# Splitting the next weight unit ahead of the sums of one, in the first 52 units of a two-layer encoder

## The chip, the cores and the metric

The kernel runs on one core of one Trainium2 chip. The time is the device time of one execution in microseconds (us); of several executions the median is given. The core has a matrix engine (TensorE, PE in the profile), VectorE (DVE), ScalarE (ACT), GpSimd (POOL) and SyncE (SP). Each works through its own queue of instructions in order; semaphores hold an instruction until what it needs is done. In this kernel SyncE issues every load and store.

## The reference

Two layers on 256 tokens of width 2048. Each layer normalises its input, scales and shifts it by a vector made from a condition `c` (the modulation), and runs a mixer; then it normalises and modulates again and runs a gated MLP with a short convolution. Cut to what matters here:

```python
mod = c_act @ ada_w[l] + ada_b[l]                       # 6 vectors of 2048
sh_a, sc_a, gt_a, sh_m, sc_m, gt_m = split(mod, 6)
h = rmsnorm(x, norm_mix[l]) * (1.0 + sc_a) + sh_a
qa, ka, va, qb, kb, vb, ga, gb = split_cols(h @ w_in[l])
ya = window_attention(...) @ w_proj_a[l]
yb = neighbourhood_attention(...) @ w_proj_b[l]
merged = sigmoid(ga) * ya + sigmoid(gb) * yb
x = x + gt_a * (merged @ w_out[l])
```

Everything is float32. The output is x after both layers.

## The kernel before

**Weights as a stream.** The matrices are cut into blocks of 128 x 128 and laid out in the order in which they are used. Sixteen blocks are a *unit*: one transfer of 1 MB into one of four `raw` buffers (`unit`, L275 on; the load is L279). A product of float32 accuracy is made from two rounded parts of each operand: ScalarE casts the unit to a high part, half a unit at a time (L288), VectorE subtracts to get the low part (L289), both into one of four `hl` buffers, each half a unit. TensorE then does three matmuls for a block: high by high, high by low, low by high (L297 to L299 for sums by features, L355 to L357 for sums by tokens). A raw buffer is free again after the second subtraction, an hl buffer after its last matmul.

**The modulation.** One row of 128 outputs is one transfer of 1 MB (L219) into the same four raw buffers (three of the first rows have a place of their own, `OWN`) and one VectorE reduction (L220). Rows come in the order of `ADA_ORDER`: shift and scale of one kc, 128 of the 2048 channels, follow each other, so that two rows give what one kc of the first `h` needs. `done[0]` counts rows. `normed` (L427 to L432) then makes one kc of h: a product on VectorE (`ht`, L427), the high part on ScalarE (L430), the low part on VectorE (L431).

**The first layer's start.** Query, key and value need all 16 kc of h, but h comes kc by kc. So the 9 token sums (groups of 512 columns) and the 16 gate sums are done in three parts, each over the kc's that `K_ENDS` gives: a part's sums are put into `packs` or `ya` in the first part (ScalarE copies, L790 and L827) and added to them in the later ones (VectorE, L792 and L822). Units 0 to 12 are part one, 13 to 34 part two, 35 to 51 part three; units 52 on belong to the projections. In the third part the finished sums are normalised (`qk_rows`: L508, L516, L531 to L533), transposed on TensorE (L540), and the heads of the attention run beside it (`attend`: L552, L556, L572, L577, L583).

**What sets the order.** The program is written in one order, and a scheduler lays it out engine by engine: earlier written work has priority, but an instruction whose inputs come late by the scheduler's reckoning is passed by others. Background work is paced: after each unit `Stream.tick` lets every job in `bg` do as many steps as its rate says. `job0` (`ada_and_h`) is such a job: its steps load a modulation row or make a kc of h; its rate is `FIRST_RATE`, one for each part. `have_h` forces it on where a sum needs a kc that is not yet written. From unit 38 on `plan` fetches later rows at the pace of `ADA_PLAN_0`. `Stream.prefetch` writes a unit's load and split before it is its turn; before the change it does so for unit 0 and at the ends of later stages.

Of the kernel before, what the change touches and what calls it, by code (L numbers as in the profile page):

```python
# [19 lines left out]
KC = D // P  # L20
HEAD = 128
HA, GA, HB = 8, 2, 8
# [15 lines left out]


K_ENDS = [  # L40
    [([2, 2, 2, 3, 3, 4, 4, 4, 4], 6), ([8, 8, 9, 10, 10, 11, 10, 10, 12], 13), ([KC] * 9, KC)],
    [([KC] * 9, KC)],
]

# [14 lines left out]
ADA_PLAN_0 = [(38, 32), (58, 48), (76, 66), (84, 70), (98, 80), (108, 80), (231, 143)]  # L59
ADA_PLAN_1 = [(8, 143), (76, 166), (84, 168), (99, 176), (108, 176), (128, 184), (142, 192)]  # L60

FIRST_RATE = [1.1, 0.85, 0.7]
ENDING = 15

WARM_IN = [8, 12, 6]
# [64 lines left out]
def encoder(ctx: ExitStack, tc: tile.TileContext, a: dict, out: bass.AP):  # L130
# [69 lines left out]
    mods, amods, nrms, done = {}, {}, {}, {0: 0, 1: 0}  # L200
# [73 lines left out]
    def unit(l, u):  # L274

        raw = rawp.tile([P, UB * P], F32, name=f"w{l}_{u}", tag="raw")
        nc.sync.dma_start(raw[:], a["ws"][l, u])  # L279
        halves = []  # L280
        streamed = any(m == "w_in" and mo < GATE_A // P for m, _, mo in STREAMS[l][u * UB : (u + 1) * UB])
        at = OFF if streamed else 0
        for j in range(2):
            n = UB * P // 2
            hl = hlp.tile([P, 2 * n + ROW], F32R, name=f"hl{l}_{u}_{j}", tag="hl")
            hl = hl[:, at : at + 2 * n].rearrange("p (a n) -> p a n", a=2)
            r = raw[:, j * n : (j + 1) * n]
            nc.scalar.copy(hl[:, 0], r)  # L288
            nc.vector.tensor_tensor(out=hl[:, 1], in0=r, in1=hl[:, 0].bitcast(F32), op=ALU.subtract)  # L289
            halves.append(hl)  # L290
        return halves
# [9 lines left out]
    class Stream:  # L301
# [16 lines left out]
        def next_block(self):  # L318
            if self.at == UB:
                if self.ahead:  # L320
                    self.halves = self.ahead.popleft()
                else:
                    self.halves = unit(self.l, self.u)
                self.u, self.at = self.u + 1, 0
            j = self.at
            self.at += 1
            return self.halves[j // 8], j % 8
# [108 lines left out]
    def first_h(h):  # L436

        rbs = spread(roots(mean_sq), WARM_IN[2])
        yield from normed(0, 0, h, rbs)
# [60 lines left out]
    def qk_rows(pss, heads, rot, gain, dst, then):  # L500

        cols = 0
        n = heads * HEAD
        ss = sm.tile([P, 8], F32, name="qss", tag="qss")
        for t, ps in enumerate(pss):
            sq = at.tile([P, 512], F32, name="qsq", tag="qsq", bufs=1)
            nc.scalar.activation(out=sq[:, :n], in_=ps[:, cols : cols + n], func=AF.Square)
            nc.vector.tensor_reduce(  # L508
                out=ss[:, t * heads : (t + 1) * heads], in_=sq[:, :n].rearrange("p (h d) -> p h d", d=HEAD), axis=AX.X, op=ALU.add
            )  # L510
        rs = sm.tile([P, 8], F32, name="qrs", tag="qrs")
        rsqrt(rs[:, : 2 * heads], ss[:, : 2 * heads], HEAD, 2 * heads)
        def norm():
            qn = at.tile([P, 2, 4, HEAD], F32, name="qn", tag="qn", bufs=1)
            for t, ps in enumerate(pss):
                nc.vector.tensor_tensor(  # L516
                    out=qn[:, t, :heads],
                    in0=ps[:, cols : cols + n].rearrange("p (h d) -> p h d", d=HEAD),
                    in1=rs[:, t * heads : (t + 1) * heads].unsqueeze(2).broadcast_to([P, heads, HEAD]),
                    op=ALU.mult,  # L520
                )
            if rot is not None:
                x1, x2 = qn[:, :, :heads, :HALF], qn[:, :, :heads, HALF:ROT]
                tab = [rot[:, i].unsqueeze(2).broadcast_to([P, 2, heads, HALF]) for i in range(4)]
                tm = []
                for i in range(2):
                    z = ev.tile([P, S], F32, name=f"rt{i}", tag="z")
                    z = z[:].rearrange("p (i t h d) -> p i t h d", i=2, t=2, h=4)
                    tm += [z[:, 0, :, :heads], z[:, 1, :, :heads]]
                for i, src in enumerate((x1, x2, x2, x1)):  # L530
                    nc.vector.tensor_tensor(out=tm[i], in0=src, in1=tab[i], op=ALU.mult)  # L531
                nc.vector.tensor_tensor(out=x1, in0=tm[0], in1=tm[1], op=ALU.subtract)
                nc.vector.tensor_tensor(out=x2, in0=tm[2], in1=tm[3], op=ALU.add)  # L533
            bg.defer(lambda: turn(qn))

        def turn(qn):
            for t in range(2):
                ps = ax.tile([P, 4, P], F32, name="qtp", tag="ax")
                for h in range(heads):
                    nc.tensor.transpose(ps[:, h], qn[:, t, h], ident[:])  # L540
                nc.scalar.activation(
                    out=dst[:, :, t * P : (t + 1) * P], in_=ps[:, :heads], func=AF.Identity, scale=gain
                )
            then()

        bg.defer(norm)
# [50 lines left out]
    def ada_all():  # L597
        yield from gens[0]
        yield from gens[1]

    adas = ada_all()
# [9 lines left out]
    def need(l, n):  # L611

        while done[l] < n:
            next(adas)

    def ada_and_h(steps):

        for kc in range(KC):
            while done[0] < 2 * kc + 1:
                next(adas)  # L620
                yield
            next(adas)
            next(steps)
            yield

    for i in range(0, KC, 4):
# [48 lines left out]
    for l in range(L):  # L675
        st = Stream(l) if l == 0 else nxt
        mod = mods.get(l)
        if l == 0:
            h = led("h0_0")
            job0 = ada_and_h(first_h(h))  # L680
            while done[0] < 2:
                next(job0)
            st.prefetch(1)
            while done[0] < 2 * K_ENDS[0][0][0][0]:
                next(job0)
            mod = mods[0]
            bg.add(job0, FIRST_RATE[0])

# [19 lines left out]
        kTa, qTa = packs[0][:, 0:3:2], packs[0][:, 4:12]  # L708
# [61 lines left out]

        def have_h(part):

            while l == 0 and done[0] < 2 * part.stop:
                next(job0)

        for pi, (groups, gates) in enumerate(parts):
            last = pi == len(parts) - 1
            if l == 0:
                bg.pace(job0, FIRST_RATE[pi])
            for g, part in enumerate(groups):  # L780
                have_h(part)
                pss = st.tokens(h, part)
                if pi == max(0, len(parts) - 2) and g == 0:
                    gains, sink, cw, rots = small(l)
                dst = packs[g // 3][:, 4 * (g % 3) : 4 * (g % 3) + 4]
                rows = dst.rearrange("p (t a) s -> p t (a s)", t=2)
                if not last or pi > 0:
                    for t, ps in enumerate(pss):
                        if pi == 0:
                            nc.scalar.copy(rows[:, t], ps[:])  # L790
                        else:
                            nc.vector.tensor_tensor(out=rows[:, t], in0=ps[:], in1=rows[:, t], op=ALU.add)  # L792
                    pss = [rows[:, t] for t in range(2)]
                if not last:
                    continue

                def have(g=g):
                    ready[0] = g + 1

                vcol = {0: GA * HEAD, 4: 0, 7: 0}.get(g)  # L800
                if vcol is not None and pi == 0:
                    for t in range(2):
                        nc.scalar.copy(rows[:, t, vcol:], pss[t][:, vcol:])
                if g == 0:
                    qk_rows(pss, GA, rots[1], gains[:, 1:2], kTa, have)
                elif g < 3:
                    qk_rows(pss, 4, rots[0], gains[:, 0:1], dst, have)
                elif vcol is None:
                    qk_rows(pss, 4, None, gains[:, 3:4] if g in (3, 6) else gains[:, 2:3], dst, have)
                else:  # L810
                    have()
                if g == 2:
                    bg.add(job, ATT[l])


            have_h(gates)
            for mo in range(BARE[0] if l else 0, KC):

                def gate_a(ps):
                    src = ps  # L820
                    if pi > 0:
                        nc.vector.tensor_tensor(out=ya[:, mo], in0=ps, in1=ya[:, mo], op=ALU.add)  # L822
                        src = ya[:, mo]
                    if last:
                        nc.scalar.activation(out=ya[:, mo], in_=src, func=AF.Sigmoid)
                    elif pi == 0:
                        nc.scalar.copy(ya[:, mo], ps)  # L827

                st.features([hs[k] for k in gates], [gate_a])
# [223 lines left out]
```

## Time and profile before

| | |
|---|---|
| Time, median of 3 executions | 2702.55 us (2701.57 to 2703.78) |
| Time of the profiled execution | 2700.72 us |
| Its span, first to last instruction | 2698.9 us |
| Granted TensorE clock, mean | 0.997 |
| Bytes moved | 700.38 MB, 260 GB/s over the span |

The span in 40 equal slices of 67.5 us, from the page. A digit is the busy share of a slice in tenths; DMA is the mean share of the 16 DMA engines, the row under it what they moved. Units 0 to 28 run in the first three slices.

```profile
PE   8999999999999999999999999999999999999999
DVE  8897888897987888788886666658878866655664
DMA  8986678987677788788756656667847775555554
GB/s 348 351 337 242 228 271 327 354 302 265 235 298 292 284 303 285 291 298 289 297 210 255 240 203 239 226 245 253 295 176 283 296 259 193 189 202 188 191 199 141
```

How to read the views used below: a row of a wait list has who waited, for whom, the sum in us, how often, and the longest. A timeline row has the start and the length in us, the engine, the line, the tiles and, in brackets, the idle time before it and what ended that. A row of a group ends with its count, busy time in us, mean length in ns, and the idle time before its instructions.

### The profile page before, as it was taken

How to read it: one execution, taken by the hardware profiler on the slowest of the kernel's cores; microseconds unless marked ns; L12 is line 12 of the kernel's file. 1: busy time of each engine (PE TensorE's matmuls, PEld its weight loads, DVE VectorE, ACT ScalarE, POOL GpSimd, SP SyncE). 2: the span in 40 equal slices, each digit the busy share in tenths (PEclk: the TensorE clock that was granted, in tenths of full speed). 3: DMA queues.
4: the chain of work that ended last, by engine and by line, in shares of the span. 5: the costliest groups of instructions: out<-in, count | busy, mean ns of one | idle time of the engine just before them, and what ended most of it. 6: DMA issues, size and time to landing. Idle time of an engine off the chain costs nothing.

```text
span 2698.9 us, 50255 instructions
## 1 busy us (share of the span) xinstructions
PE 2665.7 (99%) x21128; PEld 2565.9 (95%) x21128; DVE 2089.7 (77%) x2909; ACT 1405.0 (52%) x2078; POOL 32.6 (1%) x24
## 2 busy tenths in 40 slices
PE   8999999999999999999999999999999999999999
PEld 5879799999999999999998889999999999999999
DVE  8897888897987888788886666658878866655664
ACT  4434685445753455355564556555565445543553
POOL 0000100000000000000000000000000000000000
PEclk9999999999999999999999999999999999999999
DMA  8986678987677788788756656667847775555554
GB/s 348 351 337 242 228 271 327 354 302 265 235 298 292 284 303 285 291 298 289 297 210 255 240 203 239 226 245 253 295 176 283 296 259 193 189 202 188 191 199 141
DMA packets 101892, 700.38 MB, mean 260 GB/s; under 512 B 12705, under 2 KB 15009, under 8 KB 17697
## 3 DMA queue, kind: packets, MB, share of 16 engines
q1 hardware_dynamic: 101666, 697.17, 69.9%
q8 instruction: 165, 2.70, 0.4%
q14 instruction: 61, 0.50, 0.1%
HBM read 695.03 MB, written 2.10 MB: 258 GB/s over the span
## 4 chain that ended last, share of the span: by engine, by line
PE 86%; DVE 8%; ACT 2%; DMA 2%; issue 2%; POOL 1%; SPq 0%; DVEq 0%; ACTq 0%; POOLq 0%
PE ps L297 25%; PE ps L299 25%; PE ps L298 25%; PE ps_t L356 3%; PE ps_t L357 3%; PE ps_t L355 3%; DVE hl L289 3%; DVE aw L220 2%; DMA aw<-in_aw 1%; ACT hl L288 1%; PE po L583 1%; PE sc L552 1%; POOL qrs L402 1%; PE tp L577 0%; DVE qn L516 0%
## 5 line engine op out<-in xcount | busy, mean ns | idle before, releaser
L289 DVE TENSOR_TENSOR hl<-w,hl 128x1024 fp32r<-128x1024 f32 x928 | 1130.0, 1222 | 376.0 <-ACT hl L288 374.8
L288 ACT CAST hl<-w 128x1024 fp32r<-128x1024 f32 x928 | 969.6, 1049 | 732.8 <-PE ps L299 493.9
L297 PE MATMUL ps<-h,hl 128*128 128x256 f32 x3328 | 923.6, 278 | 3.1 <-ACT hl L288 3.1
L299 PE MATMUL ps<-h,hl 128*128 128x256 f32 x3328 | 919.5, 277 | 1.3 <-DVE hl L289 1.3
L298 PE MATMUL ps<-h,hl 128*128 128x256 f32 x3328 | 920.6, 277 | 0.0
L297 PEld LDWEIGHTS ps<-h,hl 128*128 128x128 f32 x3328 | 625.6, 188 | 4.5 <-ACT hl L288 4.1
L299 PEld LDWEIGHTS ps<-h,hl 128*128 128x128 f32 x3328 | 624.8, 188 | 1.8 <-DVE hl L289 1.7
L298 PEld LDWEIGHTS ps<-h,hl 128*128 128x128 f32 x3328 | 625.5, 188 | 0.3
L220 DVE CUSTOM_DVE_ANT_0 aw<-aw,cact,ab 128x2048 f32<-128x2048 f32 x189 | 443.6, 2348 | 55.1 <-DMA aw<-in_aw 54.4
L355 PE MATMUL ps_t<-hl,h 128*128 128x512 f32 x576 | 226.0, 399 | 9.2 <-ACT h L430 4.6
L356 PE MATMUL ps_t<-hl,h 128*128 128x512 f32 x576 | 228.2, 396 | 3.8 <-DVE hl L289 3.3
L357 PE MATMUL ps_t<-hl,h 128*128 128x512 f32 x576 | 226.6, 394 | 0.0
L898 DVE SCALAR_TENSOR_TENSOR u<-ps,cw,u 128x255 f32<-128x255 f32 x304 | 146.2, 481 | 65.4 <-ACT u L896 61.1
L896 ACT ACTIVATE u<-ps,cw 128x256 f32<-128x256 f32 x152 | 85.6, 563 | 182.8 <-PE ps L299 182.6
L299 PE MATMUL ps<-merged,hl 128*128 128x256 f32 x512 | 141.6, 277 | 0.8 <-DVE hl L289 0.8
L298 PE MATMUL ps<-merged,hl 128*128 128x256 f32 x512 | 141.5, 276 | 0.0
L297 PE MATMUL ps<-merged,hl 128*128 128x256 f32 x512 | 141.5, 277 | 0.0
L298 PE MATMUL ps<-act_o,hl 128*128 128x256 f32 x512 | 141.4, 276 | 0.0
L299 PE MATMUL ps<-act_o,hl 128*128 128x256 f32 x512 | 141.3, 276 | 0.0
L297 PE MATMUL ps<-act_o,hl 128*128 128x256 f32 x512 | 141.2, 276 | 0.0
L355 PEld LDWEIGHTS ps_t<-hl,h 128*128 128x128 f32 x576 | 108.6, 189 | 34.2 <-ACT hl L288 6.9
L356 PEld LDWEIGHTS ps_t<-hl,h 128*128 128x128 f32 x576 | 109.2, 190 | 30.9 <-DVE hl L289 8.4
(213 smaller groups left out, 4562.2 us busy)
## 6 DMA issues: line engine op xcount, KB each, us to landing
w<-in_ws SPq DMA_DIRECT2D x464, 1024.0 KB, 4.9
aw<-in_aw SPq DMA_DIRECT2D x189, 1024.0 KB, 6.1
bias<-in_bias SPq DMA_DIRECT2D x16, 256.0 KB, 4.8
x<-in_xT SPq DMA_DIRECT2D x4, 512.0 KB, 5.4
aw_o<-in_aw SPq DMA_DIRECT2D x2, 1024.0 KB, 13.3
out<-x SPq DMA_DIRECT2D x16, 128.0 KB, 2.4
aw_b<-in_aw SPq DMA_DIRECT2D x1, 1024.0 KB, 15.1
cw<-in_cw SPq DMA_DIRECT2D x2, 176.0 KB, 6.0
```

What stands on the lines that cost most here:

```text
L220: nc.vector.tensor_tensor_reduce(out=raw[:], in0=raw[:], in1=cact[:], scale=1.0, scalar=ab[:, i : i + 1], op0=ALU.mult, op1=ALU.add, accum ...
L288: nc.scalar.copy(hl[:, 0], r)
L289: nc.vector.tensor_tensor(out=hl[:, 1], in0=r, in1=hl[:, 0].bitcast(F32), op=ALU.subtract)
L297: nc.tensor.matmul(out, hi, act[0], start=first, stop=False)
L298: nc.tensor.matmul(ps[:, :S], hi, act[1], start=False, stop=False)
L299: nc.tensor.matmul(out, lo, act[0], start=False, stop=last)
L355: nc.tensor.matmul(ps[:], xh, hi, start=kc == kcs[0], stop=False)
L356: nc.tensor.matmul(ps[:], xh, lo, start=False, stop=False)
L357: nc.tensor.matmul(ps[:], xl, hi, start=False, stop=kc == kcs[-1])
L402: nc.gpsimd.tensor_tensor(out=dst, in0=src, in1=mhalf[:, :k], op=ALU.pow)
L896: nc.scalar.activation(out=u, in_=ps, func=AF.Identity, scale=w[:, 1:2], bias=w[:, 3:4])
L898: nc.vector.scalar_tensor_tensor(out=u[:, to], in0=ps[:, of], scalar=w[:, j : j + 1], in1=u[:, to], op0=ALU.mult, op1=ALU.add)
```

## The change

Three things are altered, all in the first layer's start.

1. `Stream.next_block` writes, as a unit of the first 52 begins, load and split of the unit after it (`prefetch(1)`), ahead of the unit's own matmuls and of what follows them.
2. `ada_and_h` takes three steps for a kc instead of two: row, row, h. Before, h was made in the same step as its second row. A new count, `have`, says how many kc of h are written; `have_h` and the start go by it instead of by `done`. The rates of the three parts go from 1.1, 0.85, 0.7 to 1.2, 1.0, 1.0.
3. The ends of the second part in `K_ENDS` move. A local function is renamed from `have` to `turned`.

```diff
-    [([2, 2, 2, 3, 3, 4, 4, 4, 4], 6), ([8, 8, 9, 10, 10, 11, 10, 10, 12], 13), ([KC] * 9, KC)],
+    [([2, 2, 2, 3, 3, 4, 4, 4, 4], 6), ([7, 7, 9, 9, 9, 10, 10, 11, 12], 13), ([KC] * 9, KC)],
...
-FIRST_RATE = [1.1, 0.85, 0.7]
+FIRST_RATE = [1.2, 1.0, 1.0]
+
+LEAD = 52
...
                 self.u, self.at = self.u + 1, 0
+                if self.l == 0 and self.u < LEAD:
+                    self.prefetch(1)
...
+    have = [0]
+
     def ada_and_h(steps):
 
         for kc in range(KC):
-            while done[0] < 2 * kc + 1:
+            while done[0] < 2 * kc + 2:
                 next(adas)
                 yield
-            next(adas)
             next(steps)
+            have[0] = kc + 1
             yield
...
-            while done[0] < 2:
+            while have[0] < 1:
                 next(job0)
             st.prefetch(1)
-            while done[0] < 2 * K_ENDS[0][0][0][0]:
+            while have[0] < K_ENDS[0][0][0][0]:
                 next(job0)
...
-            while l == 0 and done[0] < 2 * part.stop:
+            while l == 0 and have[0] < part.stop:
                 next(job0)
```

More of the change, by code (lines that the diff above doesn't have):

```diff
@@ L795, in encoder, with turned @@
                     continue
-                def have(g=g):
+                def turned(g=g):
                     ready[0] = g + 1
@@ L804, in encoder @@
                 if g == 0:
-                    qk_rows(pss, GA, rots[1], gains[:, 1:2], kTa, have)
+                    qk_rows(pss, GA, rots[1], gains[:, 1:2], kTa, turned)
                 elif g < 3:
-                    qk_rows(pss, 4, rots[0], gains[:, 0:1], dst, have)
+                    qk_rows(pss, 4, rots[0], gains[:, 0:1], dst, turned)
                 elif vcol is None:
-                    qk_rows(pss, 4, None, gains[:, 3:4] if g in (3, 6) else gains[:, 2:3], dst, have)
+                    qk_rows(pss, 4, None, gains[:, 3:4] if g in (3, 6) else gains[:, 2:3], dst, turned)
                 else:
-                    have()
+                    turned()
                 if g == 2:
```

## The prediction

> **What bounds the kernel now.** The page comes first: how much of the span TensorE works, and what the chain that ended last is made of.
>
> ```profile
> span 2698.9 us, 50255 instructions
> PE 2665.7 (99%) x21128; PEld 2565.9 (95%) x21128; DVE 2089.7 (77%) x2909; ACT 1405.0 (52%) x2078; POOL 32.6 (1%) x24
> ...
> PE 86%; DVE 8%; ACT 2%; DMA 2%; issue 2%; POOL 1%; SPq 0%; DVEq 0%; ACTq 0%; POOLq 0%
> ```
>
> TensorE sets the time; the change removes no matmul, so it can win only where TensorE waits. The waits of TensorE by line, from 21 us to 210 us and from 206 us to 400 us, show where:
>
> ```profile
> PE ps_t L355 <- ACT h L430: 4.6, 1, 4.6
> PE ps_t L355 <- ACT hl L288: 4.6, 6, 1.9
> PE ps_t L356 <- DVE hl L289: 3.3, 4, 1.5
> PE ps L297 <- ACT hl L288: 3.1, 3, 2.6
> PE ps L299 <- DVE hl L289: 1.3, 2, 0.8
> ...
> PE qtp L540 <- DVE qn L533: 2.5, 1, 2.5
> PE tp L577 <- ACT p L572: 2.4, 5, 1.0
> ```
>
> All but the first of the first five are waits for the split of a weight unit. I cut the first layer's start into stages at the first matmul of a unit. A unit takes 24 matmuls of 512 columns (token sums) or 48 of 256 (gate sums), so the timeline of TensorE, counted from the first such matmul at 21.37 us, gives unit 1 at 34.63, unit 10 at 92.15, unit 28 at 199.42, unit 29 at 206.22 and unit 36 at 244.33 (the last two are bounds of the stages below):
>
> ```profile
> 29.57 0.80 PE L355 MATMUL ps_t<-hl,h 128*128 128x512 f32 x1 [4.61 <-ACT h L430]
> ...
> 34.63 0.62 PE L355 MATMUL ps_t<-hl,h 128*128 128x512 f32 x2
> ...
> 92.15 0.41 PE L297 MATMUL ps<-h,hl 128*128 128x256 f32 x1 [2.61 <-ACT hl L288]
> ...
> 199.42 0.38 PE L297 MATMUL ps<-h,hl 128*128 128x256 f32 x1 [0.30 <-ACT hl L288]
> ```
>
> The busy times of these stages (columns: length, then busy time and count of PE, weight loads, DVE, ACT, POOL; granted clock, DMA share, GB/s):
>
> ```profile
> 21.37:34.63 13.26, 8.43 (x24) 5.86 (x25) 13.19 (x13) 4.01 (x6) 0.00 (x0) 0.74 0.92 380
> 34.63:206.22 171.59, 160.91 (x842) 134.02 (x840) 154.50 (x183) 77.48 (x103) 0.00 (x0) 0.99 0.89 339
> 206.22:244.33 38.11, 38.11 (x315) 37.15 (x314) 23.67 (x39) 14.75 (x14) 0.00 (x0) 1.00 0.62 221
> 244.33:362.00 117.67, 112.84 (x593) 94.51 (x591) 107.07 (x201) 78.92 (x145) 14.44 (x7) 0.99 0.65 236
> ```
>
> Units 29 to 35 run with no gap: 38.11 / 7 = 5.444 us a unit. Units 1 to 28 take 171.59 us where 28 x 5.444 = 152.4 would do: 19.2 us are lost, and there VectorE is 90% busy and the transfers 89%. That is because all 32 modulation loads of the first normalisation, each a 1 MB transfer and a VectorE reduction, stand in the queues ahead of unit 28. Behind that none follows up to unit 38, and VectorE idles for 14.44 us of 38.11. The 19.2 us are what this change can reach; unit 0 loses about 7.8 more (13.26 less 5.444), nearly all in the 4.61 us wait for the second h.
>
> SyncE, which issues all loads, waits in that stage (16 to 206 us) for buffers that VectorE gives back:
>
> ```profile
> SPq L279 <- DVE hl L289: 59.5, 18, 5.1
> SPq L219 <- DVE mod L220: 30.0, 8, 11.0
> SPq L279 <- DVE mod L220: 25.4, 7, 6.1
> ```
>
> So VectorE and the transfers bound it together, through four raw buffers.
>
> **The change, part by part.** No instruction is added or lost; the compiled order of every engine differs only up to about unit 60, and from there to the end the rows are the same. What is gained or lost by then stays.
>
> *Rate and order of the modulation loads.* A kc now takes three background steps for two. At 1.2, 1.0, 1.0 steps a unit that is 0.40, 0.33, 0.33 kc a unit for 0.55, 0.43, 0.35; the unit ahead also puts its load in front of the loads of the tick. In the compiled order of the load queue the modulation loads ahead of unit 12 fall from 18 to 16, ahead of unit 18 from 23 to 20, ahead of unit 28 from 32 to 26; all 32 are out ahead of unit 35 instead of unit 28. I bound the new loss from both queues.
>
> By transfers: unit 10 begins with 11 units, 16 modulation loads and the 2 MB of x ahead, 29 loads, and waits for them at 92.15; unit 28 with 29 + 32 + 2 = 63 at 199.42. That is 107.27 / 34 = 3.155 us a load. Afterwards unit 12 has 13 + 16 + 2 = 31 ahead: 92.15 + 2 x 3.155 = 98.5, where gap-free TensorE would be at 34.63 + 11 x 5.444 = 94.5. Loss 4.0. Unit 18 (41 loads, 130.0 against 127.2) and unit 35 (70, 221.5 against 219.7) lose less, and unit 28 (57, 180.5 against 181.6) none. Gain by this bound: 19.2 - 4.0 = 15.2.
>
> By VectorE: to unit 36 the same work is due in both kernels, 154.50 + 23.67 = 178.2 us. At the share it reached while it was pressed (154.50 / 171.59 = 0.900) it needs 198.0 us from 34.63, so unit 36 starts at 232.6; gap-free it would be at 34.63 + 35 x 5.444 = 225.2. Loss 7.4, against 244.33 - 225.2 = 19.1 now. Gain 11.7. I take this one, the tighter.
>
> *The split ahead.* The two casts and two subtractions of unit u+1 now stand ahead of unit u's evictions, and of the reductions of that tick. Behind a cast that waits for a late transfer ScalarE's copies of sums to packs queue up; TensorE waits for those through its four PSUM banks. The list of waits above has none on such a copy. I cost it at nothing: a cast that is late because of its load holds back the next unit anyway. Uncovered it would cost at most one unit, 5.4 us, once or twice. It adds no reach by itself: the raw pool and the hl pool keep four buffers each.
>
> *h a step behind.* The h of kc 1 now precedes the reduction of the fifth modulation row instead of following it; the wait at 29.57 is for the hi half, whose inputs keep their place: 0, at best 2.4 us (one reduction). Later h's come after two subtractions, 2 x 1.22 us later; the rows of VectorE for 21 to 206 us, and of ScalarE's h for 20 to 360 us:
>
> ```profile
> L289 DVE TENSOR_TENSOR hl<-w,hl 128x1024 fp32r<-128x1024 f32 x61 | 72.3, 1220 | 7.7 <-ACT hl L288 7.6
> L220 DVE CUSTOM_DVE_ANT_0 aw<-aw,cact,ab 128x2048 f32<-128x2048 f32 x27 | 63.3, 2347 | 0.7 <-DMA aw<-in_aw 0.6
> L427 DVE SCALAR_TENSOR_TENSOR ht<-x,amod,rbs 128x256 f32<-128x256 f32 x15 | 7.3, 484 | 0.5
> L431 DVE SCALAR_TENSOR_TENSOR h<-ht,mod,h 128x256 fp32r<-128x256 f32 x15 | 7.2, 482 | 4.6 <-ACT h L430 4.6
> ...
> L220 DVE DVE_READ_ACCUMULATOR2_ANT mod<- 128x1 f32 x30 | 2.5, 83 | 0.0
> L227 DVE SCALAR_TENSOR_TENSOR amod<-mod,nrm 128x1 f32<-128x1 f32 x15 | 2.4, 158 | 0.4
> ...
> L430 ACT ACTIVATE h<-ht,mod 128x256 fp32r<-128x256 f32 x16 | 8.1, 509 | 42.0 <-DVE ht L427 42.0
> ```
>
> The tightest place is unit 7, whose first gate sum takes kc 5. The compiled order puts that block's matmuls after 42 others (42 x 0.113 = 4.8 us), longer than reduction, ht and h (2.35 + 0.08 + 0.16 + 0.48 + 0.5 = 3.6): 0.
>
> *Ends of the second part.* Token sums 14 units for 15 in part two, 15 for 14 in part three; the count of sums and adds is the same: 0. But units 28 to 35 now carry six reductions and three h's: 6 x (2.347 + 0.083) + 3 x (0.158 + 0.484 + 0.482) = 18.0 us, 3.5 more than the 14.44 idle. VectorE so enters the attention stage later against TensorE. There one transposition already waits for it:
>
> ```profile
> 275.34 1.06 PE L540 MATMUL qtp<-ident,qn 128*128 128x128 f32 x8 [2.49 <-DVE qn L533]
> ...
> 276.71 0.63 PE L357 MATMUL ps_t<-hl,h 128*128 128x512 f32 x1
> ...
> 280.12 0.39 PE L356 MATMUL ps_t<-hl,h 128*128 128x512 f32 x1
> ```
>
> After it, eight starts of matmuls take 3.41 us (276.71 to 280.12) where eight of 5.444 / 24 = 0.227 take 1.82: 1.6 us, so this wait costs 4.1 in all. One modulation reduction (2.43) moves from before to after it, so it grows by 3.5 - 2.43 = 1.1, with the clock's share 1.8. Bounds: it vanishes (+4.1) or doubles (-4.1).
>
> [...]
>
> Sum: 11.7 - 1.8 = 9.9 us. The profiled execution took 2700.72 (span 2698.9), 1.8 under the median of the three runs, 2702.55; a shift applies to either: 2702.55 - 9.9, **2692.6 us**.
>
> **The rivals.** *Only the transfers bind.* VectorE can do 13.19 us in 13.26 (first stage), so 0.90 may be no ceiling. Gain 15.2, with the transposition's 4.1 up to 19.3: 2683.2 to 2687.3.
>
> *No reach, no gain.* Four raw and four hl buffers stay, and now TensorE, VectorE and the transfers are all near full at once in units 13 to 36, so each slip of one stalls the others. For: SyncE's 59.5 us for hl releases above. Against: in units 29 to 35 the same buffers fed TensorE without a gap. If VectorE's share falls to 0.85, 178.2 / 0.85 = 209.6, unit 36 stands at 244.3 as today: 2702.5 to 2704. [...]
>
> *VectorE enters attention without its lead (slower).* Between units 36 and 52 seven groups of transpositions and the eight heads of mixer A wait on VectorE in TensorE's own order; VectorE is 91% busy (107.07 of 117.67). Before, the idle of units 29 to 35 gave a lead. At 4.1 us each, from three further waits (12.3) on the gain is gone; with five it is 2702.5 - 11.7 + 20.5 = 2711. Against: only one of the fifteen waited over 1.0 us so far, and the splits now come before the adds.
>
> **How the numbers follow.** A change under 0.2% (5.4 us) can't be told from none. Forecast 0.52 (own range 2687 to 2698); transfers alone 0.14; no gain 0.19; slower 0.15. The first two are faster by over 0.2% (under 2697.1) and 0.03 of the third: 0.69. Same: the rest of the third, 0.16, and 0.01 of the last: 0.17. Slower: 0.14. The range, 2684 to 2706, takes in the forecast with its own range, nearly all of the first rival and of no gain, and leaves out most of the last.
>
> **What would show it.** Right: unit 29 starts near 195 us instead of 206.22, unit 36 near 232; TensorE's waits on lines of the split fall from 12.3 us to some 5; transfers and VectorE stay near 0.9 up to unit 36 instead of dropping at 200 us; the h wait at 29.57 stays. Wrong: waits for h at units 7 or 34 to 36; more than three new waits of qtp or tp on VectorE after unit 36; or unit 36 still at 244, with SyncE waiting as long for hl as now.

## The result, and the profile after

| | before | changed |
|---|---|---|
| median of 4 executions each | 2702.95 us (2701.57 to 2703.78) | 2688.87 us (2686.91 to 2691.95) |
| the profiled execution, its span | 2700.72, 2698.9 | 2689.0, 2687.2 |

The ratio of the times is 0.9949, with a 95% interval of 0.9932 to 0.9967: the changed kernel is 14 us faster, between 9 and 18. The profiled pair differs by 11.7 us. The page of the changed kernel, its span, busy times, transfers by slice and the summary of the chain that ended last:

```profile
span 2687.2 us, 50247 instructions
PE 2664.6 (99%) x21128; PEld 2569.8 (96%) x21128; DVE 2088.3 (78%) x2909; ACT 1401.4 (52%) x2076; POOL 33.4 (1%) x24
DMA  8987688985787878777766656666848765555554
GB/s 339 346 327 286 237 305 329 337 313 221 281 289 290 300 290 292 295 283 284 291 218 245 250 207 228 233 255 252 294 169 290 295 253 190 198 194 189 195 197 142
...
PE 79%; DVE 8%; DMA 8%; issue 3%; ACT 1%; POOL 1%; SPq 0%; DVEq 0%; ACTq 0%; POOLq 0%
```

TensorE is busy as long as before (2664.6 us for 2665.7); only the span around it is shorter. Nothing is read from the last line: TensorE has 79% of the chain here and had 86% before, but a second profile of the changed kernel gives it 88%. The fourth slice (202 to 269 us) moves 286 GB/s for 242: loads that stood ahead of unit 28 now come later. The stages by TensorE's first matmuls of units 0, 1, 29, 36 and 52, and then the second and third of them cut again at units 12 and 28 (columns as in the prediction: length, busy time and count of PE, weight loads, DVE, ACT, POOL, then granted clock, DMA share, GB/s):

```profile
22.59:35.88 13.29, 8.48 (x24) 6.01 (x25) 12.19 (x12) 4.94 (x7) 0.00 (x0) 0.74 0.90 351
35.88:194.80 158.92, 156.98 (x865) 136.29 (x864) 141.07 (x167) 75.34 (x99) 0.00 (x0) 0.99 0.88 333
194.80:233.98 39.18, 39.18 (x291) 37.29 (x289) 35.21 (x46) 16.03 (x17) 0.00 (x0) 1.00 0.88 335
233.98:349.81 115.83, 111.14 (x589) 93.05 (x588) 105.66 (x199) 76.11 (x138) 15.67 (x7) 1.00 0.66 239
...
35.88:101.55 65.67, 63.73 (x385) 56.25 (x384) 55.91 (x63) 35.53 (x55) 0.00 (x0) 0.97 0.88 332
101.55:189.15 87.60, 87.60 (x434) 74.39 (x433) 81.03 (x98) 37.71 (x43) 0.00 (x0) 1.00 0.89 336
189.15:233.98 44.83, 44.83 (x339) 42.94 (x337) 39.34 (x53) 18.14 (x19) 0.00 (x0) 1.00 0.87 331
```

Units 1 to 28 take 158.92 us for 171.59; at 28 x 5.444 = 152.4 without a gap the loss is 6.5 us for 19.2. The last three rows say where the loss is: 11 units up to unit 12 take 65.67 for 59.9, a loss of 5.8; the next 16 take 87.60 for 87.1 and have no gap at all (PE busy 87.60), while VectorE is busy 81.03 / 87.60 = 92.5% and the transfers 89%. The waits of TensorE up to 210 us and from 200 to 400 us:

```profile
PE ps_t L359 <- ACT h L434: 4.6, 1, 4.6
...
PE ps_t L359 <- ACT hl L290: 2.3, 3, 1.1
PE ps_t L360 <- DVE hl L291: 0.8, 1, 0.8
...
PE ps L299 <- ACT hl L290: 0.2, 1, 0.2
...
PE qtp L544 <- DVE qn L537: 2.8, 2, 1.8
PE tp L581 <- ACT p L576: 1.8, 3, 1.0
PE ps L301 <- DVE hl L291: 0.3, 1, 0.3
```

The four lines of waits for a split (12.3 us before) are three with 3.3 us. The wait for the second h, 4.6 us in unit 0, stays. In the attention stage the transpositions wait 2.8 us in two places, where there were 2.5 in one, and `tp` 1.8 for 2.4 (both windows end at 400 us). SyncE's waits for buffers, 16 to 195 us:

```profile
SPq L281 <- DVE hl L291: 50.6, 14, 8.7
SPq L221 <- DVE hl L291: 44.9, 13, 5.5
SPq L281 <- DVE mod L222: 27.4, 10, 6.8
```

SyncE still spends most of its time so, though TensorE waits a quarter as long: its queue is held for the same four buffers, but what stands in it is in another order. Set against before, the changed kernel is 1.2 us late at unit 0, 11.4 us early at unit 29, 10.3 at unit 36, 12.4 at unit 60, and 11.7 at the end. The chain of waits that ends at 240 us, by line, of the kernel before and then of the changed one:

```profile
by line: DVE aw L220 12.2%; DVE hl L289 10.6%; PE ps_t L356 9.9%; PE ps_t L357 9.3%; PE ps_t L355 8.8%; DMA aw<-in_aw 7.7%; PE ps L299 7.4%; PE ps L297 7.3%; PE ps L298 7.1%; issue 5.7%; ACT hl L288 4.1%; DVE aw_o L220 1.9%; DVE ht L427 1.6
```

```profile
by line: PE ps_t L360 18.2%; PE ps_t L359 18.0%; PE ps_t L361 17.6%; PE ps L299 10.0%; PE ps L301 9.9%; PE ps L300 9.8%; ACT hl L290 2.1%; DVE hl L291 2.0%; DVE aw_o L222 1.9%; PE warm L375 1.8%; DMA x<-in_xT 1.7%; issue 1.1%; DVE sq_in L64
```

Before, the chain went through reductions, splits and modulation loads, and TensorE had 50% of it; after, TensorE has 83% (71% in the second profile of the changed kernel). That chain of before names VectorE ahead of the loads; the experiments speak against reading this as the bound.

### The profile page after: what moved, and what is told of

It reads as the page before. It is cut to its first block, busy times and chain, and to the rows that moved or that the text cites. A ratio compares the mean times of both kernels' runs of the same rounds, so it can differ in the third digit from the quotient of the medians.

```text
span 2687.2 us, 50247 instructions
## 1 busy us (share of the span) xinstructions
PE 2664.6 (99%) x21128; PEld 2569.8 (96%) x21128; DVE 2088.3 (78%) x2909; ACT 1401.4 (52%) x2076; POOL 33.4 (1%) x24
## 4 chain that ended last, share of the span: by engine, by line
PE 79%; DVE 8%; DMA 8%; issue 3%; ACT 1%; POOL 1%; SPq 0%; DVEq 0%; ACTq 0%; POOLq 0%
PE ps L299 21%; PE ps L301 21%; PE ps L300 21%; DMA aw<-in_aw 7%; PE ps_t L360 4%; PE ps_t L359 4%; PE ps_t L361 4%; DVE hl L291 3%; DVE aw L222 2%; PE po L587 1%; PE sc L556 1%; ACT hl L290 1%; POOL qrs L406 1%; PE tp L581 1%; DVE qn L520 0%
```

## The experiments

One table for all of them. Unit 1 and unit 29 are the starts of TensorE's first matmul of the unit in the profile; "lost" is their distance less 152.4 us. Medians stand beside that of the kernel before on the same chip. Each "lost" is from one profile; the changed kernel, profiled twice, gave 6.5 and 5.8. Behind unit 64 the profiles scatter by more than that: half_bytes takes 2253.5 us from there to its end and before 2247.6, though TensorE, ScalarE and VectorE have the same order there in both. So what a kernel gains by its end is read from the medians.

| kernel | unit 1 | unit 29 | lost | median, before | ratio (95%) |
|---|---|---|---|---|---|
| before | 34.6 | 206.2 | 19.2 | | |
| changed | 35.9 | 194.8 | 6.5 | 2688.87, 2702.95 | 0.9949 (0.9932 to 0.9967) |
| change_again | 34.4 | 192.6 | 5.8 | 2688.83, 2700.42 | 0.9952 (0.9939 to 0.9964) |
| lead_alone | 34.7 | 203.1 | 16.0 | 2703.75, 2702.62 | 0.9997 (0.9987 to 1.0007) |
| pace_alone | 34.4 | 199.2 | 12.4 | 2699.99, 2702.62 | 0.9988 (0.9978 to 0.9999) |
| h_step | 36.6 | 201.4 | 12.4 | 2699.57, 2702.57 | 0.9981 (0.9968 to 0.9993) |
| no_lead | 36.5 | 197.0 | 8.1 | 2696.47, 2702.62 | 0.9974 (0.9963 to 0.9985) |
| old_ends | 34.9 | 196.6 | 9.2 | 2692.67, 2702.57 | 0.9959 (0.9945 to 0.9973) |
| old_pace | 34.3 | 208.9 | 22.2 | 2706.70, 2702.62 | 1.0009 (0.9997 to 1.0022) |
| half_bytes | 36.1 | 196.4 | 7.8 | 2694.87, 2702.57 | 0.9969 (0.9954 to 0.9983) |
| half_reduction | 31.1 | 203.1 | 19.6 | 2701.86, 2702.57 | 0.9997 (0.9985 to 1.0010) |
| after_half_bytes | 37.6 | 191.1 | 1.1 | 2685.08, 2700.42 | 0.9939 (0.9921 to 0.9957) |
| after_half_reduction | 30.8 | 190.4 | 7.2 | 2686.35, 2700.42 | 0.9944 (0.9926 to 0.9962) |
| own5 | 36.0 | 195.1 | 6.6 | 2690.10, 2700.42 | 0.9957 (0.9944 to 0.9971) |

### One part alone

**lead_alone**: the kernel before, with the split ahead.

```diff
                 self.u, self.at = self.u + 1, 0
+                if self.l == 0 and self.u < 52:
+                    self.prefetch(1)
```

> The kernel before with the split of the next unit written ahead in units 0 to 51, nothing else. Theory A (what counts is how many modulation loads stand ahead of a unit): they fall by one or none (31 for 32 ahead of unit 28), so at most one load, 3.2 us, is gained in units 1 to 28: 2699 to 2703. Rival B (what counts is that splits stand ahead of evictions and reductions on ScalarE and VectorE): nearly the whole gain of the change, 10 us or more: 2689 to 2693.

Unit 29 comes 3.1 us earlier, about one load of 3.155 us: in the load queue 31 modulation rows stand ahead of unit 28, where 32 did. By unit 60 only 0.3 of that is left, and the time is the same as before.

**pace_alone**: the kernel before, with the changed kernel's kc's a unit (0.4, 0.33, 0.33) at two steps a kc.

```diff
-FIRST_RATE = [1.1, 0.85, 0.7]
+FIRST_RATE = [0.8, 0.667, 0.667]
```

> The kernel before with the rates 0.8, 0.667, 0.667, which for its two steps a kc is the kc pace of the changed kernel (0.40, 0.33, 0.33 a unit); nothing else. 27 modulation loads stand ahead of unit 28 instead of 32. Theory A: 10 to 13 us faster, 2690 to 2693, unit 29 at 194 to 196 us. Rival B: under 3 us faster, 2700 to 2703, unit 29 still at 203 or later.

Rows ahead of unit 28 fall from 32 to 27, and the loss from 19.2 to 12.4. Unit 29 comes 7 us earlier where the load theory gave 10 to 12, and the time falls by 2.6 us where it gave 10 to 13; that is no more than the rival allowed. So the number of loads ahead is not all. By the prediction's count unit 14, with 35 loads ahead, is the tightest: 92.15 + 6 x 3.155 = 111.1, where gap-free TensorE is at 34.4 + 13 x 5.444 = 105.2; that would be a loss of 6, and twice that is lost.

**old_pace**: the changed kernel, with the kc's a unit of before.

```diff
-FIRST_RATE = [1.2, 1.0, 1.0]
+FIRST_RATE = [1.65, 1.275, 1.05]
```

> The changed kernel with the rates 1.65, 1.275, 1.05, which for its three steps a kc is the kc pace of the kernel before. 32 loads stand ahead of unit 28 again. Theory A: the gain is lost but for 0 to 4 us, 2699 to 2703. Rival B: the gain stays, 2687 to 2692.

All of the gain is gone: 32 rows ahead of unit 28 again, a loss of 22.2, and a time at or above that of before (theory A left 0 to 4 us of the gain). Without the slower rate the rest of the change is worth nothing.

### One part taken out

**no_lead**: the changed kernel without the split ahead.

```diff
-LEAD = 52
+LEAD = 0
```

> The changed kernel without the split ahead (units 0 to 51 split in their turn). 27 loads ahead of unit 28. Theory A: loses 0 to 3 us of the change's 14: 2689 to 2693. Rival B: loses 10 or more: 2699 or later.

The time, 2696.47 us, lies between the two forecasts. In the stage 8.1 us are lost for 6.5. At unit 36 it is 8.2 us ahead of before, at unit 52 still 8.3, but at unit 64 5.3 and at the end 3.0; the changed kernel is 10.3, 14.0, 12.4 and 11.7 ahead. The distance of the two grows from 2.1 to 8.7 us. The waits of TensorE in no_lead from 225 to 440 us:

```profile
PE tp L581 <- ACT p L576: 3.9, 4, 1.2
PE qtp L544 <- DVE qn L537: 3.0, 3, 1.1
PE ps L301 <- DVE hl L291: 2.6, 3, 1.4
```

The changed kernel's in that window are 1.8, 2.8 and 0.3, as listed above. That is 9.5 us against 4.9: 4.6 of the 5.0 us by which the distance of the two grows from unit 36 (2.1) to unit 64 (7.1). So the split ahead earns more behind unit 36 than in the stage for which it was costed: 2.3 us in waits for a late subtraction, 2.1 in waits for `p`. How it shortens them was not followed further, and the 1.6 us that come behind unit 64 are within the scatter there.

**old_ends**: the changed kernel with the ends of before. **h_step**: the same, and without the split ahead, so that only the rate and the step of h are changed.

```diff
-    [([2, 2, 2, 3, 3, 4, 4, 4, 4], 6), ([7, 7, 9, 9, 9, 10, 10, 11, 12], 13), ([KC] * 9, KC)],
+    [([2, 2, 2, 3, 3, 4, 4, 4, 4], 6), ([8, 8, 9, 10, 10, 11, 10, 10, 12], 13), ([KC] * 9, KC)],
...
-LEAD = 52
+LEAD = 0
```

> The changed kernel with the old ends of the second part. If the ends only spread the same sums differently, as the prediction has it, 2688 to 2692 as the change; if they are a condition of the gain, 2694 or more.

> The kernel before with h one step behind its rows and the new rates: no split ahead, old ends. It differs from pace_alone (same kc pace, 7.0 us earlier at unit 29) by the step alone. If the step is worth nothing, as the prediction has it, unit 29 is 6 to 8 us earlier than before and the time is as pace_alone's, 2697 to 2700; if it brings the 11 us that the change without its split ahead had gained from unit 1 to unit 29, unit 29 is 9 to 11 us earlier and the ends bring nothing there.

h_step loses 12.4 us, exactly what pace_alone does: the step of h is worth nothing. (Its unit 29 is 4.8 us earlier than before's, not 6 to 8, since unit 1 starts 1.9 us later.) The ends are worth 12.4 - 8.1 = 4.3 us in the stage without the split ahead (h_step against no_lead), and 9.2 - 6.5 = 2.7 with it; in the whole time the intervals of those pairs overlap, and old_ends, at 2692.67 us, lies between its two forecasts. Two things make up 3.8 of the 4.3 us. The old ends ask for kc's earlier, and so the load queue has one modulation row more ahead of units 18 and 19 in h_step (21 and 22) than in no_lead (20 and 21), and likewise one more ahead of units 19 and 20 in old_ends than in the changed kernel; h_step loses 2.0 us in units 18 and 19, where no_lead loses none (one row more also stands ahead of units 21, 22 and 24, where neither loses). The other is unit 16, which takes 7.24 us in h_step and 5.44 in no_lead. VectorE's timeline in h_step, with an add of sums, the split behind it, and the matmul of TensorE that waits for that split:

```profile
126.24 1.37 DVE L798 TENSOR_TENSOR packA<-ps_t,packA 128x512 f32<-128x512 f32 x2 [2.25 <-PE ps_t L361]
127.52 2.35 DVE L291 TENSOR_TENSOR hl<-w,hl 128x1024 fp32r<-128x1024 f32 x2
...
128.80 0.50 PE L360 MATMUL ps_t<-hl,h 128*128 128x512 f32 x1 [1.47 <-DVE hl L291]
```

and the same add in no_lead:

```profile
122.62 1.37 DVE L798 TENSOR_TENSOR packA<-ps_t,packA 128x512 f32<-128x512 f32 x2 [0.22 <-PE ps_t L361]
```

The add stands ahead of the split in VectorE's queue and waits 2.25 us for sums that TensorE hasn't finished; the split behind it is late, and TensorE then waits 1.47 for that. With the new ends the sums are done 0.22 us after VectorE gets there. This reading of the 1.8 us rests on the two traces; the order of add and split was not changed by itself.

### Which resource binds

**half_bytes** and **half_reduction** cut one cost each in the kernel before, for the first 32 rows. The first loads half a row and reduces it twice, so that VectorE's work stays; the second loads all of it and reduces half.

```diff
+            halves = 2 if l == 0 and n < 2 * KC else 1
+            cols = D // halves
-            nc.sync.dma_start(raw[:], a["aw"][l, n])
+            nc.sync.dma_start(raw[:, :cols], a["aw"][l, n][:, :cols])
+            for k in range(halves):
...
+                    out=raw[:, :cols], in0=raw[:, :cols], in1=cact[:, k * cols : (k + 1) * cols], scale=1.0,
```

```diff
+            cols = D // 2 if l == 0 and n < 2 * KC else D
-                out=raw[:], in0=raw[:], in1=cact[:], scale=1.0, scalar=ab[:, i : i + 1],
+                out=raw[:, :cols], in0=raw[:, :cols], in1=cact[:, :cols], scale=1.0, scalar=ab[:, i : i + 1],
```

> The kernel before, but each of the first 32 modulation rows loads only its first half (0.5 MB for 1 MB) and VectorE reduces that half twice, so that its work stays what it was (two instructions of half the length for one). The sums lack the second half. If the transfers are what holds units 1 to 28 back, 16 MB less stand ahead of unit 28 (47 loads for 63) and the loss of 19.2 us nearly goes: unit 29 at 187 to 192 instead of 206.22. If VectorE holds them back, unit 29 stays at 202 to 208.

> The kernel before, but VectorE reduces only the first half of each of the first 32 modulation rows, which are loaded whole. The sums lack the second half. VectorE has some 33 us less to do by unit 28 (29 x 1.15). If VectorE holds units 1 to 28 back, unit 29 comes at 187 to 192; if the transfers do, at 199 to 206, since 63 loads at 3.1 us still stand ahead of unit 28.

The row of units 1 to 28 of half_bytes:

```profile
36.08:196.36 160.28, 156.26 (x842) 132.78 (x840) 150.12 (x238) 75.37 (x103) 0.00 (x0) 1.00 0.78 274
```

and of half_reduction:

```profile
31.07:203.09 172.02, 161.15 (x841) 134.50 (x840) 129.90 (x183) 77.59 (x104) 0.00 (x0) 0.99 0.91 344
```

With half the bytes the loss falls from 19.2 to 7.8 us and the time by 0.31%, with the same 32 rows ahead of unit 28; unit 29 starts at 196.4 us, not as early as the 187 to 192 expected. VectorE then works 150.12 / 160.28 = 93.7%. With half the reduction VectorE's share falls to 129.90 / 172.02 = 75.5%, and nothing is gained: 19.6 lost, the transfers at 0.91 and 344 GB/s (unit 29 is 3.1 us earlier than before's only because unit 1 is, by 3.6). So VectorE's share of 90% was not what held units 1 to 28 back in the kernel before: 24.6 us less of its work there gained nothing. That the transfers through four buffers did is what half_bytes points to, but it is not shown alone. Both edits change lengths that the scheduler reckons with, and with them the order: up to some 200 us the orders of ScalarE and VectorE differ from before's in some 15 to 25 places each, and half_bytes also has its small loads elsewhere in SyncE's queue. A run with half the bytes in the old order is missing. For what binds next there is only a chain, up to 240 us of half_bytes, with VectorE at its head, and such a chain misled before:

```profile
by line: DVE hl L292 21.8%; DMA w<-in_ws 18.8%; DVE aw L223 15.6%; issue 7.7%; PE ps L300 4.7%; PE ps L302 4.6%; PE ps L301 4.6%; ACT hl L291 3.1%; DVE aw_o L223 2.0%; DVE packB L795 2.0%; DMA x<-in_xT 1.7%; DVE ht L430 1.6%; DMA bias<-in_b
```

**after_half_bytes** and **after_half_reduction** are the same two edits in the changed kernel.

> The changed kernel, but each of the first 32 modulation rows loads only its first half and VectorE reduces that half twice (the sums lack the second half). In the kernel before, this took the loss of units 1 to 28 from 19.2 us to 7.9. If in the changed kernel VectorE is the tighter bound, as the prediction has it, the loss (6.5 us up to unit 29, 7.6 up to unit 36) stays at 5 to 9; if transfers still are, it falls under 3.

> The changed kernel, but VectorE reduces only the first half of each of the first 32 modulation rows, which are loaded whole (the sums lack the second half). In the kernel before, this left the loss of units 1 to 28 at 19.6 us. If VectorE is the tighter bound in the changed kernel, the loss of 6.5 up to unit 29 falls under 4; if transfers are, it stays at 5 to 8.

Here the two don't part so well. By the loss it is the bytes again: 1.1 us with half of them, 7.2 with half the reduction, both as forecast for transfers. But the starts of unit 1 lie 6.8 us apart (37.6 and 30.8), since the early reductions are shorter in the one (1.28 us each with the same edit in half_reduction, 2.35 whole), and unit 29 starts at the same place in both (191.1 and 190.4), 1.4 to 4.4 us ahead of the changed kernel's two profiles. The whole times are 2 to 4 us under 2688.83, for both, from two executions each. So little is left in this stage that no one cut brings much, the order moves with these edits too, and which of the two binds in the changed kernel stays open.

### What is left at unit 3, and the change once more

**own5**: the changed kernel, with a place of its own for the sixth modulation row, so that the load of unit 3 needn't wait for that row's buffer.

```diff
-OWN = {2: "o", 3: "o", 4: "b1"}
+OWN = {2: "o", 3: "o", 4: "b1", 5: "b0"}
```

> The changed kernel with a place of its own for the sixth modulation row (in the room of packB_0, which is not written before unit 2), so that the load of unit 3 takes the raw buffer of unit 0 instead of that of unit 1. If late loads make the 4 us that the changed kernel still loses in units 2 and 3, unit 4 starts 2 to 4 us earlier than its 56.28 and the time is 2 to 4 us below the change's; if h makes them, or if the transfers at the start are full anyway, no more than 1 us.

Unit 3's load is issued at 25.05 us in own5, by SyncE's timeline, where in the changed kernel it is at 34.08:

```profile
25.05 0.33 SPq L281 DMA_DIRECT2D w<-in_ws  x1
```

```profile
34.08 0.33 SPq L281 DMA_DIRECT2D w<-in_ws  x1
```

ScalarE's timeline, own5 first, then the changed kernel:

```profile
46.62 0.59 ACT L796 COPY packB<-ps_t 128x512 f32<-128x512 f32 x1 [2.94 <-PE ps_t L361]
47.10 1.99 ACT L290 CAST hl<-w 128x1024 fp32r<-128x1024 f32 x2
```

```profile
46.48 0.59 ACT L796 COPY packB<-ps_t 128x512 f32<-128x512 f32 x1 [2.94 <-PE ps_t L361]
46.97 1.99 ACT L290 CAST hl<-w 128x1024 fp32r<-128x1024 f32 x2
```

A load 9 us earlier moves the cast by nothing. In both the cast follows a copy of sums that waited 2.94 us for TensorE. Unit 4 starts at 56.43 us, as late as in the changed kernel (56.28), and ScalarE's and VectorE's orders are the same. So the load isn't what delays unit 3; the order of ScalarE's queue, copy ahead of cast, fits. after_half_bytes supports it: there the first cast for unit 3 stands ahead of the copies (it starts at 43.40 us, they at 44.35), and units 2 and 3 take 5.51 us each, almost without loss. But that run's loads are shorter too; the order was not changed by itself. The time is that of the changed kernel.

**change_again**: the changed kernel as it is, beside these runs.

> The changed kernel itself, beside own5 on the same chip: 2687 to 2692 again; its first profile started unit 0 1.2 us later than before's, for which nothing in the order gives a cause, so unit 0 may start at 21.4 this time.

The ratio repeats (0.9952); between the medians it is 11.6 us here, where it was 14.1. Unit 0 starts at 21.2 us in this profile, so the 1.2 us by which it was late in the first is scatter, and this profile ends 15.0 us ahead of that of before.

## Why the prediction was right, and where it was not

**The stage and its size: right.** The 19.2 us lost in units 1 to 28 were what could be had, and about 13 of them were gained (12.7 and 13.4 in the two profiles). Unit 29 was put near 195 us and started at 194.80, unit 36 near 232 and started at 233.98; waits for splits fell to 3.3 us where some 5 were expected; the transfers stayed at 0.88 up to unit 36; the h wait stayed.

**The bound: wrong, though its number came out.** The step that failed is "Loss 7.4 ... Gain 11.7. I take this one, the tighter": VectorE at 0.900 of its time as the ceiling. It worked 92.5% from unit 12 to unit 28 of the changed kernel without TensorE waiting once, and 93.7% in half_bytes; and halving its reductions brought nothing in half_reduction. The loss isn't spread over units 1 to 35, as such a ceiling would have it: up to unit 36 it is 7.6 us, 5.8 of them by unit 12, 0.5 in the next 16 units, 1.3 in the last 8 (44.83 us for 43.55). That is the shape of the other sum, by transfers, whose 4.0 us also fell due by unit 12 (as an argument from shape: the pair of runs on the changed kernel left its bound open); the second profile of the changed kernel lost 5.0 there. But 3.9 of the 5.8 (2.7 of the 5.0) were lost in units 2 and 3 alone, where own5 shows that an earlier load doesn't help, so that sum isn't shown right either. The likeness of 7.4 and 7.6 is chance.

**The rival "only the transfers bind"** is borne out for the kernel before in so far as half of VectorE's reductions gained nothing and half of the bytes 11.4 us, the latter in another order; its time, 2683.2 to 2687.3, lies just under the median of 2688.87.

**The rate of the loads: half of it right.** The whole gain of the stage was put to it. Alone it brings 6.8 of 12.7 us. Taken away, it costs everything. It is needed, but doesn't suffice: fewer loads ahead only help if the splits aren't then late for another reason.

**"I cost it at nothing ... It adds no reach by itself" (the split ahead): wrong with the rest of the change, right without.** By itself it brought 3.1 us that were gone by unit 60. In the changed kernel it is 1.6 us in the stage and 7.1 by unit 64, 5.0 of them behind unit 36, where the prediction gave it no part at all. In the whole time no_lead gains 6.2 us on before and the changed kernel 11.6 or 14.1, so it is 5.4 to 7.9, though the intervals of the ratios just touch (no_lead's begins at 0.9963, the changed kernel's end at 0.9967 and 0.9964).

**"Token sums 14 units for 15 in part two ...: 0" (the ends): wrong in the stage**, 2.7 to 4.3 us, since they decide how soon a modulation row is asked for and which adds stand ahead of a split. The count of sums, which the step went by, doesn't show either. In the whole time their worth is not told apart from none.

**h a step behind: 0, as predicted.**

**The attention stage: wrong sign.** It was to cost 1.8 us, the bounds being 4.1 either way. From unit 36 to unit 64 the changed kernel gained 2.1 us in both profiles (1.4 and 2.4 to the end). The `qtp` wait did go from 2.5 to 2.8 us, but TensorE's waits for `p` fell, and the clock's share went: behind the 2.49 us wait of before the granted clock is 0.72 over the 6 us from 275 us on, which is 1.7 us, and from unit 36 to 420 us of the changed kernel it is 1.00, though a `qtp` wait there took 1.79 us. That may be luck in part: at unit 3 the same two waits left the clock at 0.79 in one profile of the changed kernel and at 1.00 in the other. The slower rival lived in this stage and was priced at 20.5 us; what the orders tried here moved between units 36 and 64 lies between -2.9 (no_lead) and +2.4 us (old_pace).

**No reach, no gain** fell. It leant on SyncE's long waits. TensorE's waits for splits went from 12.3 to 3.3 us with the same four buffers, by an order that loads less ahead, and in half_bytes the loss went from 19.2 to 7.8 us by smaller loads, in another order. That more buffers would have done the same isn't excluded; it was not tried.

The sum was 9.9 us where 14.1 were measured between the medians, and 11.7 and 15.0 between profiles: 11.7 for the stage was near, though by a ceiling that doesn't hold, and most of the rest is the attention's 1.8 of the wrong sign and the 1.4 to 2.4 gained behind unit 36 instead.

## What to carry to other kernels

Two engines near 90% don't tell which one binds, and neither does a chain of waits that passes through both: halve the work of one and leave the other's, and see whether the loss moves, but compare the orders as well: where a scheduler lays them out, such a cut changes more than the work. Count how many loads stand ahead of each unit in the one queue that issues them; but a queue relieved of loads only pays if the in-order queues behind it don't put an instruction that waits for TensorE ahead of one that TensorE waits for (in h_step an add that waited 2.25 us stood ahead of a split for which TensorE then waited 1.47). Parts that are worth little alone (in the whole time nothing for the split ahead and 2.6 us for the rate; the ends were not tried alone) can be worth 12 to 14 together, so a part costed at nothing should be taken out of the whole before it is called idle.

## What the runs showed of the hardware

**Behind the same two waits under 1 us the clock was 0.79 in one profile and 1.00 in another.** In unit 3 of the changed kernel TensorE waited 0.94 and then 0.77 us, and the matmuls behind started 0.43 us apart:

```profile
48.07 0.49 PE L359 MATMUL ps_t<-hl,h 128*128 128x512 f32 x1 [0.94 <-ACT hl L290]
49.33 0.80 PE L360 MATMUL ps_t<-hl,h 128*128 128x512 f32 x1 [0.77 <-DVE hl L291]
49.92 0.63 PE L361 MATMUL ps_t<-hl,h 128*128 128x512 f32 x1
50.35 0.63 PE L359 MATMUL ps_t<-hl,h 128*128 128x512 f32 x1
```

In change_again the same two waits, to the hundredth, were followed by starts 0.23 us apart:

```profile
46.51 0.49 PE L359 MATMUL ps_t<-hl,h 128*128 128x512 f32 x1 [0.94 <-ACT hl L290]
47.77 0.50 PE L360 MATMUL ps_t<-hl,h 128*128 128x512 f32 x1 [0.77 <-DVE hl L291]
48.11 0.39 PE L361 MATMUL ps_t<-hl,h 128*128 128x512 f32 x1
48.34 0.40 PE L359 MATMUL ps_t<-hl,h 128*128 128x512 f32 x1
```

Over unit 3 the granted clock was 0.79 in the one and 1.00 in the other, and the unit took 8.2 and 7.0 us. In own5 the two waits are the same again, and the starts behind them 0.43 us apart (50.04 and 50.46 us). Longer waits went both ways too: behind the `qtp` wait of 2.49 us in before the granted clock was 0.72 over 6 us, behind that of 1.79 us in the changed kernel, which ended at 263.39 us, it was 1.00 over 6 us. What decides between the two these runs don't show.

**Matmuls of 256 columns came at two paces, 0.118 and 0.113 us, at one and the same granted clock, 1.00.** Gate sums started 0.118 us apart through units 27 to 33 of the changed kernel (granted clock 1.00 in that stage), and 0.113 apart in units 29 to 34 of before (1.00 as well). The changed kernel, then before:

```profile
200.10 0.28 PE L299 MATMUL ps<-h,hl 128*128 128x256 f32 x1
200.22 0.28 PE L300 MATMUL ps<-h,hl 128*128 128x256 f32 x1
200.34 0.28 PE L301 MATMUL ps<-h,hl 128*128 128x256 f32 x1
```

```profile
211.55 0.28 PE L299 MATMUL ps<-h,hl 128*128 128x256 f32 x1
211.66 0.28 PE L297 MATMUL ps<-h,hl 128*128 128x256 f32 x1
211.77 0.28 PE L298 MATMUL ps<-h,hl 128*128 128x256 f32 x1
```

A unit so takes 5.65 us for 5.444, which is the 1.3 us of the last 8 units above. VectorE and the transfers are both busier there than they were in before's units (35.21 us in 39.18 for 23.67 in 38.11, and 0.88 for 0.62), but the traces speak against that as the cause: the pace is the same 0.118 in each of those units of the changed kernel, with the transfers at 0.97 (unit 29) and at 0.55 (unit 33) and with VectorE busy 100% (unit 27) and 73% (unit 28); and from 330.0 to 335.7 us of the changed kernel, with VectorE busy 95%, gate sums start 0.113 apart. The cause stays open.
